# Residual loads with VectorE adds in place of accumulating transfers, and one more seven-product pair, in the down projections of a YOCO trunk

## The chip, the cores and the metric

The kernel runs on one core of a Trainium2 chip. The metric is the device time of one execution in microseconds. Before the change the median of three runs is 2191.21 us (2190.79 to 2191.95). PE is TensorE, DVE is VectorE, ACT is ScalarE, POOL is GpSimd and SP is SyncE, whose queue here carries the weights.

## What is computed

A decoder trunk of two layers in float32 over 256 tokens of width 2048: gated linear attention, a gated feed-forward part with a convolution over tokens, shared keys and values, block-sparse attention, and a second feed-forward part. Each part ends with a projection that is added to the residual stream. These four projections (out of 2048 features twice, out of 5632 features twice) are what the change is about:

```python
h = h + gla_mixer(...)          # ends with  o @ w_out
h = h + conv_ffn(...)           # ends with  (jax.nn.silu(a) * u) @ w_down
h = h + moba_mixer(...)         # ends with  o @ w_out
h = h + conv_ffn(...)
```

## The kernel before

**Weights.** All weights come from DRAM once, in chunks of 1 MB (tile `wraw`, three buffers, requested on SP at L96). A chunk is used in halves of 128x1024. ACT casts each half to its high part `whi` (L140), DVE subtracts to get the low part `wlo` (L141). Each product is then three matmuls: high by high, low activations by high weights, high activations by low weights. `WeightStream.prefetch` keeps the split a few halves ahead of PE; a new chunk is requested when DVE has made the last low part of an older one.

**Down projections.** `down()` is called four times: `go` (the mixer's output), `dn0`, `mo` and `dn1`. Each call makes two column blocks of 1024 (b = 0, 1), and each block walks pairs of 128-row slices of the activations in the order that `ORDERS` gives. A plain pair takes eight 128x512 products, which are 24 matmuls. A pair marked with `+` takes seven products (21 matmuls) of combined operands, as in Strassen's scheme, into seven partial sums p1 to p8 (p[1], p[5], p[6], p[7] serve all four quarters of the result). For it, DVE makes the sums `t13` and `t24` of a chunk's quarters (`_sums`, L106 to L108), four halves (one of them 512 wide) are split in place of two, and the activations need a combination `comb`: a sum of the pair's rows (L613), four steps of 128x128 (L603 to L606), and a split by ACT (L303) and DVE (L304). Combinations are made once for both blocks. For dn0 and dn1 those of pairs 1, 3, 5, 7 are made while the pairs themselves are; the others are made in the first block that needs them, queued two pairs ahead.

**End of a block.** The pairs behind the `|` are plain and come last, first for the left 512 columns, then for the right ones (f = 0, 1). When the last seven-product pair is done, ACT copies p[1] and DVE makes the four sums that all quarters share (`r[0]` to `r[3]`, named c0 to c3, L756 to L760). Then four transfers on POOL's queue add the residual from DRAM to c0 to c3 in place (L762, `accum_op`, 256 KB each; from `x_tok` for go, from `rows1` to `rows3` for the others). During the tail, as each f is finished, DVE adds the last partial sums (L771) and `done` stores the rows (L784, on POOL; for dn1 the output, L834 on SP and ACT).

**What sets the order.** The program is laid out by a scheduler that models time; `with ws.behind()` places what is issued inside it behind the latest split. Buffers of kind `slot` come from one pool of 35 (a place of 4 KB per partition).

Of the kernel before, what the change touches and what calls it, by code (L numbers as in the profile page):

```python
# [8 lines left out]
F32 = mybir.dt.float32  # L9
# [3 lines left out]
OP = mybir.AluOpType  # L13
# [24 lines left out]
def _order(text):  # L38

    words = text.replace("|", " ").split()  # L40
    return [(int(k.rstrip("+")), k.endswith("+")) for k in words], len(text.split("|")[1].split())
# [2 lines left out]
EARLY = (1, 3, 5, 7)  # L44
ORDERS = {
    "go": [_order("0 1+ 2 3+ 4 | 5 6 7"), _order("0 2 1+ 3+ 4 | 5 6 7")],
    "dn0": [_order("0 2 4 6 8 1+ 10 3+ 12 5+ 14 7+ 16 9+ 17 11+ 18 13+ 15 | 19 20 21"),
            _order("0 2 4 6 1+ 8 3+ 10 5+ 12 7+ 14 9+ 16 11+ 13+ 18 15+ 17+ 19 | 20 21")],
    "mo": [_order("0 2 1+ 3+ 4 | 5 6 7"), _order("0 2 1+ 3+ 4 | 5 6 7")],
    "dn1": [_order("0 2 4 6 8 1+ 10 3+ 12 5+ 14 7+ 16 9+ 17 11+ 18 13+ 15 | 19 20 21"),  # L50
            _order("0 1+ 2 3+ 4 5+ 6 7+ 8 9+ 10 11+ 12 13+ 14 15+ 16 17+ 18+ | 19 20 21")],
}

# [104 lines left out]
def trunk(ctx: ExitStack, tc: tile.TileContext, xT, x_tok, cst, msk, w1p, w2a, w_k, w_qa, w_v2, w_v, w_g, w_go,  # L158
          w_up0, w_dn0, w_kk, w_kv, w_mq, w_mo, w_up1, w_dn1, rel, onehot, out):
    nc = tc.nc  # L160
    V, A, T = nc.vector, nc.scalar, nc.tensor
# [11 lines left out]
    def slot(shape, dt, name):  # L173
        return big.tile(shape, dt, name=name, tag="slot")

    def temp(name, shape=(128, 2, S), dt=F32):
        return tmp.tile(list(shape), dt, name=name, tag="temp")

    def bank(name, shape):
        return mis_ps.tile(list(shape), F32, name=name, tag="bank")  # L180
# [5 lines left out]
    ws = WeightStream(tc, raw, parts)  # L186
# [85 lines left out]
    def step():  # L272
        due = [job for at, job in later if at <= cur[0]]
        later[:] = [(at, job) for at, job in later if at > cur[0]]
        for job in due:
            job()
        halves_ = ws.get(cur[0])
        cur[0] += 1
        return halves_
# [331 lines left out]
    def combine_parts(k, xs, into):  # L611
        t = temp("whole")
        V.tensor_add(t, xs[k][:, :, :S], xs[k][:, :, S:])  # L613
        combine(k, [(t[:, i, :128], t[:, i, 128:]) for i in range(2)], into)
# [87 lines left out]
    def down(name, xs, combos, res, done, jobs):  # L702

        for b, (order, n_tail) in enumerate(ORDERS[name]):
            new = [k for k, seven in order if seven and k not in combos]
            todo = {i: list(js) for i, js in jobs.get(b, {}).items()}
            for k in new:
                at = next(i for i, (k_, _) in enumerate(order) if k_ == k)
                todo.setdefault(max(at - 2, 0), []).append(lambda k=k: combine_parts(k, xs, combos))
            low = acc_ps.tile([128, 2, 512], F32, name="acc")  # L710
            pair, single = ((3, 8), (2, 4)) if name.startswith("dn") else ((2, 3), (4, 8))
            p = {n: low[:, i] for i, n in enumerate(pair)}
            p.update({n: bank(f"p{n}", (128, 512)) for n in single})
            left = dict.fromkeys(range(1, 9), 0)
            for k, seven in order:
                for n in ((1, 5, 7, 6, 4, 3, 2) if seven else (2, 3, 4, 8, 2, 3, 4, 8)):
                    left[n] += 3
            begun = set()

            def prods(*todo):  # L720

                w = step()
                for n, _, _ in todo:
                    if n not in p:
                        two = acc_ps.tile([128, 2, 512], F32, name="acc")
                        p.update({n: two[:, 0], {1: 6, 5: 7}[n]: two[:, 1]})
                for xi, wi in ((0, 0), (1, 0), (0, 1)):
                    for n, x, f in todo:
                        left[n] -= 1
                        T.matmul(p[n], x[xi], w[wi][:, 512 * f:512 * f + 512], start=n not in begun, stop=left[n] == 0)  # L730
                        begun.add(n)

            def part(k, i, t):
                x = xs[k][:, i, 128 * t:]
                return x[:, :128], x[:, S:S + 128]

            def comb(k, f):
                return combos[k][:, f, 0], combos[k][:, f, 1]

            last = max(i for i, (k, seven) in enumerate(order) if seven)  # L740
            for i, (k, seven) in enumerate(order[:-n_tail]):
                for job in todo.get(i, ()):
                    job()
                if seven:
                    prods((1, part(k, 0, 0), 0))
                    prods((3, comb(k, 3), 0), (2, part(k, 1, 0), 1))
                    prods((5, comb(k, 0), 0), (7, comb(k, 2), 1))
                    prods((6, comb(k, 1), 0), (4, part(k, 1, 1), 1))
                else:
                    for a in range(2):  # L750
                        prods(*((n, part(k, a, t), f)
                                for n, t, f in ((2, 0, a), (3, 0, 1 - a), (4, 1, a), (8, 1, 1 - a))))
                if i == last:

                    r = [temp(f"c{n}", (128, 512)) for n in range(4)]
                    A.copy(r[0], p[1])  # L756
                    V.tensor_add(r[1], r[0], p[6])  # L757
                    V.tensor_add(r[2], r[1], p[7])
                    V.tensor_add(r[1], r[1], p[5])
                    V.tensor_add(r[3], r[2], p[5])  # L760
                    for n in (0, 2, 1, 3):
                        nc.gpsimd.dma_start(r[n], res(n // 2, 2 * b + n % 2), accum_op=OP.add)  # L762
            for f, ns in enumerate(((2, 4), (3, 8))):
                for i, (k, _) in enumerate(order[-n_tail:]):
                    for job in todo.get((f, i), ()):
                        job()
                    prods(*((n, part(k, a, t), a) for a in range(2) for t, n in enumerate(ns)))
                if f:
                    ws.prefetch(cur[0])
                for t, n in enumerate(ns):  # L770
                    V.tensor_add(r[2 * t + f], r[2 * t + f], p[n])  # L771
                    done(t, 2 * b + f, r[2 * t + f])
# [41 lines left out]
    def middle(name, xs, combos, res, nrm, keep_row, at, feature_major, parked=None):  # L814
        done, back, in_acc, in_bank = onward(nrm, keep_row, parked)
        jobs = {}
        for q, (b, i) in enumerate(at):
            jobs.setdefault(b, {}).setdefault(i, []).append(lambda q=q: back(q, in_acc))
        down(name, xs, combos, res, done, jobs)
        for q in range(len(at), NP):  # L820
            after(1 if feature_major else q - 3, lambda q=q: back(q, in_bank))
        after(2 if feature_major else 3, nrm.close)
        if feature_major:
            after(3, nrm.weave)
# [7 lines left out]
    def last_down(hid, sums):  # L832
        def done(t, c, x):
            (A if t and c % 2 else nc.sync).dma_start(out[t, :, 512 * c:512 * c + 512], x)  # L834

        down("dn1", hid, sums, rows3, done, {})
# [149 lines left out]
    for g in range(4):  # L986
# [4 lines left out]
        f = (q8[:, g % 2 * 4:g % 2 * 4 + 4], (q1[:, 0:2], q1[:, 2:4]))  # L991
# [3 lines left out]
    for g in range(4):  # L995
# [3 lines left out]
        f = (k8[:, g % 2 * 4:g % 2 * 4 + 4], [slot([128, 2, 2, S], F32R, f"k1{c}") for c in range(2)])  # L999
# [120 lines left out]
```

## Time and profile before

| what | before |
|---|---|
| median of three runs | 2191.21 us |
| profiled execution | 2188.61 us |
| its span | 2186.7 us |
| PE busy | 2170.4 us, 99% |
| DVE busy | 1597.0 us, 73% |
| ACT busy | 1284.1 us, 59% |
| POOL busy | 300.9 us, 14% |
| granted TensorE clock, mean | 0.999 |

The profiled execution takes about 2 us beyond its span and is 2.6 us shorter than the median. A matmul's row reads 0.39 us, but matmuls overlap, so the distance of their starts is what one costs. A busy share is a mean over stages: what stands still, and when, is read from the waits and the timeline. Lines are those of the kernel before.

### The profile page before, as it was taken

To read this page: it belongs to the slowest core of one execution; us is meant where nothing else is said; L and a number is where in the kernel's file an instruction comes from. 1 tells how busy PE (TensorE), PEld (TensorE's weight loads), DVE (VectorE), ACT (ScalarE), POOL (GpSimd) and SP (SyncE) were. 2 spreads that over 40 slices of the span, in tenths; PEclk is the share of its full clock that TensorE was granted. 3 is DMA by queue.
4 is the path that set the end of the run, shared out by engine and by line. 5 is a ranking of instruction groups with operands and counts; after the bars stand their busy time and mean duration, and the time that the engine had idled before them with its cause. 6 is when DMAs were issued, how large, how long until landed. Compare 5 with 4: busy or idle time off the path is not lost.

```text
span 2186.7 us, 26956 instructions
## 1 busy us (share of the span) xinstructions
PE 2170.4 (99%) x9693; PEld 1793.1 (82%) x9693; DVE 1597.0 (73%) x2202; ACT 1284.1 (59%) x1858; POOL 300.9 (14%) x448
## 2 busy tenths in 40 slices
PE   9999999999999999999999999999999999999999
PEld 7888887888888888788888888888888888887887
DVE  6655586667776777878967787776777676769887
ACT  6555765556565656555556676555656565655454
POOL 1011111111111111000023241011111111110000
PEclk9999999999999999999999999999999999999999
DMA  8466577577777787675678887676687777775655
GB/s 317 178 231 210 185 245 256 201 241 232 240 240 242 242 256 234 198 251 202 223 252 269 275 277 229 205 235 230 232 249 236 247 237 246 237 243 206 222 205 173
DMA packets 92248, 510.11 MB, mean 233 GB/s; under 512 B 13729, under 2 KB 14769, under 8 KB 42194
## 3 DMA queue, kind: packets, MB, share of 16 engines
q1 hardware_dynamic: 60722, 417.53, 54.4%
q0 software_dynamic: 30816, 90.28, 15.3%
q8 instruction: 76, 1.25, 0.2%
q10 hardware_dynamic: 576, 0.58, 0.1%
q14 instruction: 58, 0.48, 0.1%
HBM read 463.22 MB, written 45.11 MB: 232 GB/s over the span
## 4 chain that ended last, share of the span: by engine, by line
PE 85%; DMA 5%; DVE 4%; issue 4%; ACT 1%; POOL 1%; DVEq 0%; SPq 0%; ACTq 0%; POOLq 0%
PE acc L290 41%; PE acc L293 20%; PE acc L730 13%; PE p L730 9%; DVE wlo L141 2%; DMA wraw<-w_dn 1%; DMA upT<-turned 1%; DMA wraw<-w_go 1%; ACT whi L140 1%; POOL upT L667 1%; DMA turned<-z 0%; PE sT L561 0%; DMA h<-xT 0%; PE o L578 0%; DVE au L680 0%
## 5 line engine op out<-in xcount | busy, mean ns | idle before, releaser
L141 DVE TENSOR_TENSOR wlo<-wraw,whi 128x1024 fp32r<-128x1024 f32 (+1 forms) x786 | 929.7, 1190 | 398.5 <-ACT whi L140 376.7
L140 ACT CAST whi<-wraw 128x1024 fp32r<-128x1024 f32 (+1 forms) x786 | 797.2, 1026 | 604.9 <-PE acc L290 391.0
L290 PE MATMUL acc<-whi,xw 128*128 128x512 f32 x3840 | 952.9, 390 | 2.6 <-ACT whi L140 1.9
L290 PEld LDWEIGHTS acc<-whi,xw 128*128 128x128 f32 x3840 | 719.5, 188 | 154.8 <-ACT whi L140 3.8
L293 PE MATMUL acc<-wlo,xw 128*128 128x512 f32 x1920 | 514.2, 389 | 0.0
L293 PEld LDWEIGHTS acc<-wlo,xw 128*128 128x128 f32 x1920 | 360.3, 188 | 74.8
L730 PE MATMUL p<-whi,hid 128*128 128x512 f32 x572 | 204.0, 390 | 0.0
L730 PE MATMUL acc<-whi,hid 128*128 128x512 f32 x506 | 168.8, 389 | 0.0
L676 ACT ACTIVATE au<-upT,cs 128x256 f32<-128x256 f32 x176 | 96.0, 595 | 70.1 <-DMA upT<-turned 70.1
L140 ACT CAST whi<-t 128x1024 fp32r<-128x1024 f32 x82 | 85.5, 1052 | 87.5 <-PE p L730 26.8
L667 POOL DMA_DIRECT2D upT<-turned x176 | 114.3, 656 | 148.7 <-DMA turned<-z 59.5
L290 PE MATMUL acc<-whi,xkv 128*128 128x512 f32 x512 | 128.8, 391 | 0.0
L661 POOL DMA_DIRECT2D turned<-z x44 | 34.1, 776 | 676.7 <-DVE z L657 615.0
L730 PEld LDWEIGHTS p<-whi,hid 128*128 128x128 f32 x572 | 107.4, 188 | 22.7 <-ACT whi L140 0.4
L680 DVE SCALAR_TENSOR_TENSOR au<-upT,cs,au 128x255 f32<-128x255 f32 x176 | 77.4, 471 | 55.8 <-ACT au L676 55.6
L730 PEld LDWEIGHTS acc<-whi,hid 128*128 128x128 f32 x506 | 95.0, 188 | 19.6
L730 PE MATMUL acc<-whi,comb 128*128 128x512 f32 x328 | 107.6, 393 | 3.4 <-ACT whi L140 3.1
L290 PEld LDWEIGHTS acc<-whi,xkv 128*128 128x128 f32 x512 | 94.6, 188 | 18.7
L730 PE MATMUL p<-wlo,hid 128*128 128x512 f32 x286 | 106.4, 391 | 2.6 <-DVE wlo L141 2.6
L141 DVE TENSOR_TENSOR wlo<-t,whi 128x1024 fp32r<-128x1024 f32 x82 | 98.6, 1217 | 9.8 <-ACT whi L140 5.4
L730 PE MATMUL acc<-wlo,hid 128*128 128x512 f32 x253 | 92.2, 389 | 0.0
L762 POOL DMA_DIRECT2D c<-rows x24 | 21.3, 1074 | 463.4 <-DVE c L757 451.2
(251 smaller groups left out, 1956.3 us busy)
## 6 DMA issues: line engine op xcount, KB each, us to landing
wraw<-w_up SPq DMA_DIRECT2D x176, 1024.0 KB, 5.3
wraw<-w_dn SPq DMA_DIRECT2D x88, 1024.0 KB, 4.9
turned<-z POOLq DMA_DIRECT2D x44, 512.0 KB, 3.5
upT<-turned POOLq DMA_DIRECT2D x176, 128.0 KB, 5.0
wraw<-w_g SPq DMA_DIRECT2D x16, 1024.0 KB, 5.0
wraw<-w_go SPq DMA_DIRECT2D x16, 1024.0 KB, 5.4
wraw<-w_mq SPq DMA_DIRECT2D x16, 1024.0 KB, 6.6
wraw<-w_kk SPq DMA_DIRECT2D x16, 1024.0 KB, 6.0
```

What stands on the lines that cost most here:

```text
L140: one = nc.scalar.copy(hi[:, a:b], src[:, a:b])
L141: two = nc.vector.tensor_sub(lo[:, a:b], src[:, a:b], hi[:, a:b].bitcast(F32))
L290: T.matmul(ps[:, t, :], xs(kt)[:, x0 + 128 * t:x0 + 128 * t + 128], hi[:, c:c + 512], start=kt == 0 and x0 == 0, stop=False)
L293: T.matmul(ps[:, t, :], xs(kt)[:, 128 * t:128 * t + 128], lo[:, c:c + 512], start=False, stop=kt == KT - 1)
L661: nc.gpsimd.dma_start(turned[J].rearrange("(a i) r q c -> (i r) a (q c)", a=4), z.rearrange("p (a q) t c -> p a (q t c)", a=4))
L667: nc.gpsimd.dma_start(f[32 * q:32 * q + 32].rearrange("p a (i c) -> p (a i) c", i=4), turned[J][:, :, q, :].rearrange("a r c -> r a c"))
L676: A.activation(au[:, i, :], t[:, i, :], AF.Identity, bias=col(cb + n), scale=col(cw + 2 * 2 * FT + n))
L680: V.scalar_tensor_tensor(au[:, i, 1:], t[:, i, :S - 1], col(cw + 2 * FT + n), au[:, i, 1:], op0=OP.mult, op1=OP.add)
L730: T.matmul(p[n], x[xi], w[wi][:, 512 * f:512 * f + 512], start=n not in begun, stop=left[n] == 0)
L762: nc.gpsimd.dma_start(r[n], res(n // 2, 2 * b + n % 2), accum_op=OP.add)
```

## The change

It does two things. In the first blocks of dn0 and dn1 the orders end with `13+ 19 15+ | 20 21` in place of `13+ 15 | 19 20 21`: pair 15 takes seven products in the first block too, and pair 19 moves from the tail to the middle. In all eight blocks the four accumulating transfers go; two buffers `kept` receive the residual by four plain loads on POOL's queue, and DVE adds them to c0 to c3, two adds at each f, placed behind the latest split during the first tail pair.

```diff
--- before.py
+++ after.py
@@ -44,10 +44,10 @@
 EARLY = (1, 3, 5, 7)
 ORDERS = {
     "go": [_order("0 1+ 2 3+ 4 | 5 6 7"), _order("0 2 1+ 3+ 4 | 5 6 7")],
-    "dn0": [_order("0 2 4 6 8 1+ 10 3+ 12 5+ 14 7+ 16 9+ 17 11+ 18 13+ 15 | 19 20 21"),
+    "dn0": [_order("0 2 4 6 8 1+ 10 3+ 12 5+ 14 7+ 16 9+ 17 11+ 18 13+ 19 15+ | 20 21"),
             _order("0 2 4 6 1+ 8 3+ 10 5+ 12 7+ 14 9+ 16 11+ 13+ 18 15+ 17+ 19 | 20 21")],
     "mo": [_order("0 2 1+ 3+ 4 | 5 6 7"), _order("0 2 1+ 3+ 4 | 5 6 7")],
-    "dn1": [_order("0 2 4 6 8 1+ 10 3+ 12 5+ 14 7+ 16 9+ 17 11+ 18 13+ 15 | 19 20 21"),
+    "dn1": [_order("0 2 4 6 8 1+ 10 3+ 12 5+ 14 7+ 16 9+ 17 11+ 18 13+ 19 15+ | 20 21"),
             _order("0 1+ 2 3+ 4 5+ 6 7+ 8 9+ 10 11+ 12 13+ 14 15+ 16 17+ 18+ | 19 20 21")],
 }
 
@@ -752,19 +752,25 @@
                                 for n, t, f in ((2, 0, a), (3, 0, 1 - a), (4, 1, a), (8, 1, 1 - a))))
                 if i == last:
 
+                    kept = [slot([128, 2, 512], F32, "kept") for _ in range(2)]
+                    for f in range(2):
+                        for t in range(2):
+                            nc.gpsimd.dma_start(kept[f][:, t], res(t, 2 * b + f))
                     r = [temp(f"c{n}", (128, 512)) for n in range(4)]
                     A.copy(r[0], p[1])
                     V.tensor_add(r[1], r[0], p[6])
                     V.tensor_add(r[2], r[1], p[7])
                     V.tensor_add(r[1], r[1], p[5])
                     V.tensor_add(r[3], r[2], p[5])
-                    for n in (0, 2, 1, 3):
-                        nc.gpsimd.dma_start(r[n], res(n // 2, 2 * b + n % 2), accum_op=OP.add)
             for f, ns in enumerate(((2, 4), (3, 8))):
                 for i, (k, _) in enumerate(order[-n_tail:]):
                     for job in todo.get((f, i), ()):
                         job()
                     prods(*((n, part(k, a, t), a) for a in range(2) for t, n in enumerate(ns)))
+                    if i == 0:
+                        with ws.behind():
+                            for t in range(2):
+                                V.tensor_add(r[2 * t + f], r[2 * t + f], kept[f][:, t])
                 if f:
                     ws.prefetch(cur[0])
                 for t, n in enumerate(ns):
```

The scheduler moves instructions with it. On POOL, at the end of go's first block (`turned<-gates` is the last load before it, `rows_2415` the store of the block's result; c_2585 to c_2588 are c0 to c3), before:

```order
L393 DMA turned<-gates 32x4x256 x4
L762 DMA c_2585<-x_tok 128x512
L762 DMA c_2586<-x_tok 128x512
L762 DMA c_2587<-x_tok 128x512
L762 DMA c_2588<-x_tok 128x512
L784 DMA rows_2415<-c_2585 128x512
L784 DMA rows_2415<-c_2587 128x512
L784 DMA rows_2415<-c_2588 128x512
L784 DMA rows_2415<-c_2586 128x512
L762 DMA c_2942<-x_tok 128x512
```

and now (c_2591 to c_2594 are c0 to c3):

```order
L393 DMA turned<-gates 32x4x256 x4
L758 DMA kept<-x_tok 128x512 x4
L790 DMA rows_2415<-c_2591 128x512
L790 DMA rows_2415<-c_2593 128x512
L790 DMA rows_2415<-c_2594 128x512
L790 DMA rows_2415<-c_2592 128x512
L758 DMA kept<-x_tok 128x512 x4
```

The loads don't wait for DVE's sums any more and stand right behind `turned<-gates`; those of the second block stand right behind the stores of the first, with nothing of DVE's second block ahead of them.

On DVE, in the tail of go's first block (t_2662 and t_2663 are t13 and t24 of the second block's first seven-product pair), before:

```order
L141 TENSOR_TENSOR wlo<-wraw,whi 128x1024
L771 TENSOR_TENSOR c_2585<-c_2585,acc 128x512
L771 TENSOR_TENSOR c_2587<-c_2587,p_2421 128x512
L141 TENSOR_TENSOR wlo<-wraw,whi 128x1024
L771 TENSOR_TENSOR c_2588<-c_2588,p_2422 128x512
L106 TENSOR_TENSOR t_2662<-wraw 128x1024
L141 TENSOR_TENSOR wlo<-wraw,whi 128x512
L107 TENSOR_TENSOR t_2663<-t_2662,wraw 128x512
L771 TENSOR_TENSOR c_2586<-c_2586,acc 128x512
L141 TENSOR_TENSOR wlo<-wraw,whi 128x1024
```

and now (t_2666 and t_2667):

```order
L141 TENSOR_TENSOR wlo<-wraw,whi 128x1024
L773 TENSOR_TENSOR c_2591<-c_2591,kept 128x512
L773 TENSOR_TENSOR c_2593<-c_2593,kept 128x512
L141 TENSOR_TENSOR wlo<-wraw,whi 128x1024
L777 TENSOR_TENSOR c_2591<-c_2591,acc 128x512
L777 TENSOR_TENSOR c_2593<-c_2593,p_2421 128x512
L141 TENSOR_TENSOR wlo<-wraw,whi 128x1024
L773 TENSOR_TENSOR c_2592<-c_2592,kept 128x512
L773 TENSOR_TENSOR c_2594<-c_2594,kept 128x512
L106 TENSOR_TENSOR t_2666<-wraw 128x1024
L777 TENSOR_TENSOR c_2594<-c_2594,p_2422 128x512
L141 TENSOR_TENSOR wlo<-wraw,whi 128x512
```

The four adds of `kept` have come in (L773), two ahead of the first final adds (L777, before L771) and two behind the low part that follows them.

On DVE, in the first block of dn0, where combinations are made beside the splits (t_7195 and t_7196 are t13 and t24 of one chunk, t_7274 and t_7275 of the next), before:

```order
L141 TENSOR_TENSOR wlo<-t_7195,whi 128x1024
L685 TENSOR_TENSOR au<-au 128x256
L604 TENSOR_TENSOR comb<-comb,whole 128x128
L141 TENSOR_TENSOR wlo<-t_7196,whi 128x1024
L106 TENSOR_TENSOR t_7274<-wraw 128x1024
L141 TENSOR_TENSOR wlo<-wraw,whi 128x1024
L606 TENSOR_TENSOR comb<-whole,comb 128x128
L141 TENSOR_TENSOR wlo<-wraw,whi 128x1024
```

and now (t_7207 and t_7208, then t_7286):

```order
L141 TENSOR_TENSOR wlo<-t_7207,whi 128x1024
L685 TENSOR_TENSOR au<-au 128x256
L604 TENSOR_TENSOR comb<-comb,whole 128x128
L141 TENSOR_TENSOR wlo<-t_7208,whi 128x1024
L613 TENSOR_TENSOR whole<-hid 128x512
L106 TENSOR_TENSOR t_7286<-wraw 128x1024
L141 TENSOR_TENSOR wlo<-wraw,whi 128x1024
L606 TENSOR_TENSOR comb<-whole,comb 128x128
L141 TENSOR_TENSOR wlo<-wraw,whi 128x1024
```

A further sum of a pair's rows (L613, pair 15) stands between the low part of `t_7208` and the sum for the next chunk; its four small steps follow among the next splits.

## Rows read from the trace of the kernel before

**Rows 1.** Busy time, share of the span and instructions of each engine.

```profile
PE 2170.4 (99%) x9693; PEld 1793.1 (82%) x9693; DVE 1597.0 (73%) x2202; ACT 1284.1 (59%) x1858; POOL 300.9 (14%) x448
```

**Rows 2.** TensorE's waits: engine, line, waited for; us in total, times, longest us.

```profile
PE acc L730 <- ACT whi L140: 3.1, 1, 3.1
PE p L730 <- DVE wlo L141: 3.1, 4, 0.9
```

**Rows 3.** Timeline (start us, us, engine, line, operation; idle before), TensorE, tail of dn0's first block.

```profile
966.33 1.98 PE L730 MATMUL p<-whi,hid 128*128 128x512 f32 x8
...
969.05 1.98 PE L730 MATMUL p<-whi,hid 128*128 128x512 f32 x8
```

**Rows 4.** Groups by form: busy us, mean ns of one; idle before; VectorE.

```profile
L106 DVE TENSOR_TENSOR t<-wraw 128x1024 f32<-128x1024 f32 x41 | 50.0, 1220 | 27.5 <-DMA wraw<-w_dn 22.9 <-DMA wraw<-w_mo 3.1 <-DMA wraw<-w_go 1.3
...
L613 DVE TENSOR_TENSOR whole<-hid 128x512 f32<-128x512 f32 x11 | 7.5, 684 | 0.0
...
L603 DVE TENSOR_TENSOR comb<-whole 128x128 f32<-128x128 f32 x11 | 3.1, 284 | 1.9 <-DMA out_dram<-c 1.9
```

**Rows 5.** Timeline, VectorE, ScalarE and TensorE, first block of dn0, around 918 us.

```profile
917.37 1.23 DVE L106 TENSOR_TENSOR t<-wraw 128x1024 f32<-128x1024 f32 x1 [0.29 <-DMA wraw<-w_dn]
918.51 1.22 DVE L141 TENSOR_TENSOR wlo<-t,whi 128x1024 fp32r<-128x1024 f32 x1
...
917.19 1.05 ACT L140 CAST whi<-t 128x1024 fp32r<-128x1024 f32 x1 [4.19 <-DVE t L108]
...
918.73 0.39 PE L730 MATMUL acc<-whi,comb 128*128 128x512 f32 x1
```

**Rows 6.** Windows, first block of dn0: stretch, its length, VectorE busy (instructions), clock, DMA.

```profile
895.00:955.00 60.00, 58.98 (x75) 1.00 0.57 210
955.00:970.00 15.00, 10.82 (x12) 1.00 0.68 235
```

**Rows 7.** DMA queues, 318 to 330 us, then 330 to 340: packets, MB, share.

```profile
q0 software_dynamic: 576, 1.05, 55.2%
q1 hardware_dynamic: 217, 1.57, 31.3%
...
q0 software_dynamic: 320, 1.05, 27.0%
```

**Rows 8.** DMA queues 323 to 326 us; timelines of SyncE and ScalarE, first chunk.

```profile
q0 software_dynamic: 221, 0.40, 86.2%
...
322.59 0.33 SPq L96 DMA_DIRECT2D wraw<-w_go  x1
...
331.04 1.05 ACT L140 CAST whi<-wraw 128x1024 fp32r<-128x1024 f32 x1 [7.12 <-DMA wraw<-w_go]
```

**Rows 9.** Timelines of VectorE, SyncE, ScalarE, TensorE, between go's blocks.

```profile
329.06 0.69 DVE L771 TENSOR_TENSOR c<-c,acc 128x512 f32<-128x512 f32 x1 [3.61 <-PE acc L730]
...
332.12 1.23 DVE L141 TENSOR_TENSOR wlo<-wraw,whi 128x1024 fp32r<-128x1024 f32 x1 [1.78 <-ACT whi L140]
...
338.04 0.33 SPq L96 DMA_DIRECT2D wraw<-w_go  x1
...
345.36 0.62 ACT L140 CAST whi<-wraw 128x512 fp32r<-128x512 f32 x1 [4.70 <-DMA wraw<-w_go]
...
349.91 0.50 PE L730 MATMUL acc<-whi,comb 128*128 128x512 f32 x1 [3.12 <-ACT whi L140]
```

**Rows 10.** Windows, TensorE's granted clock (PEclk) behind the wait in go.

```profile
350.00:355.00 5.00, 4.88 (x14) 0.66 0.42 144
```

**Rows 11.** Timelines of SyncE, VectorE and TensorE, dn1, first to second block.

```profile
2050.76 0.33 SPq L96 DMA_DIRECT2D wraw<-w_dn  x1
...
2059.92 1.23 DVE L106 TENSOR_TENSOR t<-wraw 128x1024 f32<-128x1024 f32 x1 [3.64 <-DMA wraw<-w_dn]
...
2081.14 0.50 PE L730 MATMUL p<-wlo,hid 128*128 128x512 f32 x1 [0.81 <-DVE wlo L141]
```

**Rows 12.** DMA issues: KB each, median us to landing, chunks of the down weights.

```profile
wraw<-w_dn SPq DMA_DIRECT2D x88, 1024.0 KB, 4.9
```

## The prediction

> **What bounds the kernel now.** I read the busy shares first, then TensorE's waits, then the stretches around them. TensorE (PE) is busy 2170.4 of 2186.7 us, VectorE (DVE) 73% of the span [rows 1]. So a matmul taken out is worth its slot, and anything else pays only where PE stands still. PE's waits are few: 3.1 us once for a cast on ScalarE (ACT) and 3.1 us in four waits for a low part that DVE makes [rows 2], all of them in the down blocks, which are what is edited. Durations are those of the profiled execution (2188.61 us, of which 2186.7 are the span). The median of the runs is 2191.21, so I work out a difference and set it on the median.
>
> **1. Two plain pairs become seven-product pairs.** Each saves 24 - 21 = 3 matmuls, and the pair is walked once in dn0 and once in dn1: six matmuls. A row of a matmul reads 0.39 us, but rows overlap. In the tail of dn0's first block half a pair has 8 matmuls on high weights, the first at 966.33, then 4 on low ones, and the next half begins at 969.05 [rows 3]: 12 in 2.72 us, 0.227 us each. Six are **-1.36 us**, certain as long as PE is fed.
>
> What feeds them is dearer. By form DVE takes 0.68 us for a pass over 128x512 (the sum of a pair's rows, say), 0.28 for each of the four small steps of a combination and 1.22 for a pass over 128x1024 [rows 4]; in a row each starts some 0.08 us before the one ahead has ended (917.37 and 918.51 [rows 5]), so they count as 0.60, 0.20 and 1.14. The combination of pair 15, with its low part of 512, is 0.60 + 4 x 0.20 + 0.60 = 2.0 us. It leaves the second block and comes into the first. The seven-product form adds the sums t13 and t24 (1.14 + 2 x 0.60 = 2.3 us) and two more low parts, one of them short (1.14 + 0.60 = 1.7). How close PE is there: the high part that began at 917.19 on ACT, right after DVE had made its source, was ready at 918.24, and PE read it at 918.73, 0.49 us later [rows 5]. Of the combination, 0.60 + 3 x 0.20 = 1.2 us stand on DVE ahead of the halves that PE takes at 918 to 920. DVE has 0.29 us of idle just before, at 917.37, and in all 1.02 us in the 60 from 895 to 955, then 4.18 in 15 [rows 6], so I expect 0.9 us of lateness against 0.49 of cushion: +0.4 to +0.5 us, with 0 (the scheduler's order hides it) and +1.4 (all of it, and a little more) as bounds. Twice: **+1.0 us** (0 to +2.8). For the rest of this extra work I count nothing: the plain tail pairs need only two low parts in 5.4 us of PE, and the 4.2 idle us of 955 to 970 are their cover. If that cover isn't enough, rival B follows.
>
> **2. Accumulating transfers become plain loads and DVE adds.** Eight blocks exchange four transfers for four. The price per MB on the rings: from 318 to 330 us the four accumulates of go's first block are the 1.05 MB of the software queue, 55.2% of 12 us, 6.6 us on every ring; from 330 to 340 plain transfers of the same 1.05 MB cost 27.0% of 10 us, 2.7 us [rows 7]. So 8 MB cost some 31 us less ring time. Almost none of that is on the path: none of PE's waits names such a transfer. The 32 new adds are 0.60 us each, 2.4 us a block. Where they count:
>
> **go, first to second block.** The chain is: the chunk asked for at 322.59 moved nothing while the accumulates ran (from 323 to 326 the only packets are the 221 of the software queue), and its cast began at 331.04, 8.4 us later [rows 8]. DVE then worked without a gap from 332.12 until it freed a buffer; the next chunk was asked for at 338.04, and its cast began at 345.36, after ACT had waited 4.70 us for it; PE stood still for 3.12 us until 349.91 [rows 9]. In the next 5 us PE had a granted clock of 0.66 [rows 10], between its two levels of 1.2 and 2.4 GHz, which costs 5 x 0.34 = 1.7 us. Afterwards:
> - The first chunk lands 2 to 3 us sooner. DVE can use 1.8: in the new order the two final adds, which wait for PE until 329.06 [rows 9], stand ahead of the low part, so that it starts at 329.06 + 2 x 0.60 = 330.3 in place of 332.12. -1.8.
> - Of the four residual adds two fall into the idle 3.61 us before 329.06, two into the full stretch: +1.2. The next request comes at about 337.4.
> - The residual loads of the second block stand on GpSimd's queue right behind the last store, so they are issued at about 337 to 339 and fill the rings beside the critical chunk: 0 if they come after it, 2.7 us if all come first. I take the middle, +1.4: the rows that bound it don't say who goes first.
>
> Sum -1.8 + 1.2 + 1.4 = **+0.8 us** (-0.6 to +2.1; I stretch it to +3, since the first block's loads now fall into 306 to 318, where the rings already carry weights). The slow clock stays.
>
> The rows thus show a chunk that got no turn for three microseconds while accumulates were queued [rows 8]. The Trainium skill (DMA: Bandwidth & Descriptors, Queues, rings and completion order) says otherwise: an engine takes turns, one packet each, between the queues that have work. By that rule a chunk (217 packets for 1.57 MB, so 9 per ring and MB) would wait behind 9 plain packets of 0.135 us (27.0% of 160 us over 320), an estimate of 1.2 us, and this term would be +0.6 and not +0.8; the same rule would have let the chunk of 322.59 through, which the trace contradicts, so I keep the middle of the bounds.
>
> **mo, first block.** The same edit; its boundary has one of the four short waits, none of which is longer than 0.9 us [rows 2]. **+0.2 us**, bounds -1.3 (the wait and the steps around it go) and +1.5 (as in go, without its gain).
>
> **dn1, second block.** The accumulates of the first block hold the chunk asked for at 2050.76: DVE stands idle for it 3.64 us, until 2059.92, and is still late at 2081.14, where PE stops 0.81 us [rows 11]. With plain loads the chunk should land in about 5 us, the median of these chunks [rows 12]: **-0.8 us** (bounds -1.0 and 0; other work of DVE may keep it late).
>
> **No cost:** GpSimd's shorter issues (14% busy); the last adds of dn1, which still wait for PE's last product. If the loads came too late there, DVE's last add would show it.
>
> Sum: -1.36 + 1.0 + 0.8 + 0.2 - 0.8 = **-0.2 us**, 2188.4 for the profiled execution and **2191.0** beside the median.
>
> **Rivals.**
> A, the stall in go goes away. If the chunk asked for at 337.4 lands in 4.9 us, as chunks of the down weights do in the median [rows 12], it is there at 342.3; 4.6 us later (345.3 to 349.9) PE gets it, at 346.9, and its old block ended at 349.91 - 3.12 = 346.8 [rows 9]. Then 3.12 + 1.7 = 4.8 us go in place of +0.8: -0.2 - 5.6 = -5.8, **2185.4**. For it: the rings are nearly idle just before. Against it: 1 MB of loads is put in the same three microseconds.
>
> B, DVE becomes the bound of the first down blocks (slower). Combination 2.0, sums 2.3, low parts 1.7, adds 2.4: 8.4 us of new work against 1.02 + 4.18 = 5.2 us of idle from 895 to 970 [rows 6]. If PE's cushions there are used up, DVE ends 3.2 us late, and PE with it: 2 x (3.2 - 0.5) = +5.4 us more, +5.2 in all, **2196.4**. It decides once the lateness passes the cushion of the halves after 930. Against it: a good part of the work comes after 955, where plain pairs ask little of DVE.
>
> C, the loads of the second blocks all go before the critical chunks, in go (+2.1) and mo (+1.5): +1.3 + 1.3 more, +2.4 in all, **2193.6**: no visible change.
>
> D, the edit does nothing that shows, since PE is never short of work: -1.36 alone, 2189.9. It can't be told from the forecast.
>
> **The numbers.** A measurement of this kernel can tell 0.2%, 4.4 us: below 2186.8 is faster, above 2195.6 slower. Forecast with C and D: 0.72, spread by the bounds over 2187 to 2195.5, a little of it beyond. A: 0.15. B: 0.13. Faster 0.18, same 0.67, slower 0.15. The range goes from 2186.0 (into A) to 2195.5.
>
> **What would show it.** In the profile after: 9687 matmuls on PE in place of 9693; plain packets where the accumulates were and no weight chunk above 8 us beside them; PE's wait for ACT in go between 2.5 and 5 us, with the slow clock behind it; a wait of about half a microsecond for ACT or DVE near 919 and near 2004; no wait at 2081. Wrong would be: the gap in go gone (A), several waits for DVE between 930 and 980 (B), or a slow clock in a stretch that had none.

## The result and the profile after

The changed kernel takes 2207.64 us in the median of nine runs (2195.45 to 2215.67), the kernel before 2191.21. The ratio is 1.0071, 95% interval 1.0053 to 1.0088: slower by 0.7%. Forecast were 2191.0 us, no visible change. The profiled execution takes 2204.61 us, its span is 2202.8. The page of the changed kernel has against [rows 1]:

```profile
PE 2177.1 (99%) x9687; PEld 1794.0 (81%) x9687; DVE 1624.4 (74%) x2244; ACT 1288.9 (59%) x1862; POOL 291.4 (13%) x448
```

Six matmuls are gone, as forecast, and yet PE is busy 6.7 us longer, in part because a matmul at the slow clock is a longer row (0.79 us at 324.50 below, where the row at 320.47 before reads 0.39). TensorE's waits in the changed kernel, to be read beside [rows 2] (us in total, times, longest):

```profile
PE acc L730 <- ACT whi L140: 5.5, 5, 3.3
PE p L730 <- DVE wlo L141: 4.6, 4, 3.0
PE acc L730 <- ACT go L303: 4.1, 1, 4.1
PE acc L290 <- ACT whi L140: 3.7, 7, 0.9
```

The third didn't exist before, the second has a single wait of 3.0 where the longest was 0.9. Where the time went shows best when the same instruction is looked up in both timelines of TensorE. Before (the last row of [rows 9], at 349.91, is the first product of pair 1+ in go's second block, which has walked pairs 0 and 2 by then; then the first products of the first up projection and of dn0, one early in dn0's first block and one early in mo):

```profile
384.12 2.00 PE L290 MATMUL acc<-whi,xw 128*128 128x512 f32 x8
...
865.08 0.39 PE L730 MATMUL p<-whi,hid 128*128 128x512 f32 x1
...
901.83 0.50 PE L730 MATMUL p<-wlo,hid 128*128 128x512 f32 x1 [0.87 <-DVE wlo L141]
...
1398.49 0.50 PE L730 MATMUL p<-wlo,ox 128*128 128x512 f32 x1 [0.53 <-DVE wlo L141]
```

After, the same five:

```profile
357.08 0.50 PE L730 MATMUL acc<-whi,comb 128*128 128x512 f32 x1 [3.28 <-ACT whi L140]
...
391.06 2.00 PE L290 MATMUL acc<-whi,xw 128*128 128x512 f32 x8
...
875.58 0.39 PE L730 MATMUL p<-whi,hid 128*128 128x512 f32 x1
...
912.00 0.50 PE L730 MATMUL p<-wlo,hid 128*128 128x512 f32 x1 [0.88 <-DVE wlo L141]
...
1414.63 0.49 PE L730 MATMUL p<-wlo,ox 128*128 128x512 f32 x1 [0.53 <-DVE wlo L141]
```

They are late by 7.2, 6.9, 10.5, 10.2 and 16.1 us, and the span is 16.1 us longer. So go loses 7.2 us up to pair 1+ of its second block and wins back 0.2, the first up projection loses 3.6, dn0 and what follows it up to mo 5.6, and from mo's first block to the end nothing is lost or won.

**go.** The timelines of GpSimd, SyncE, ScalarE and TensorE in the changed kernel, and below them the clock behind the wait (stretch, length, TensorE busy, clock, DMA share, GB/s):

```profile
307.66 2.18 POOL L758 DMA_DIRECT2D kept<-x_tok  x4
...
312.61 0.33 SPq L96 DMA_DIRECT2D wraw<-w_go  x1
...
313.32 2.00 ACT L140 CAST whi<-wraw 128x1024 fp32r<-128x1024 f32 x2 [2.18 <-DMA wraw<-w_go]
318.94 1.05 ACT L140 CAST whi<-wraw 128x1024 fp32r<-128x1024 f32 x1 [3.62 <-DMA wraw<-w_go]
...
321.94 1.05 ACT L140 CAST whi<-wraw 128x1024 fp32r<-128x1024 f32 x1 [1.47 <-DVE c L761]
322.89 0.90 ACT L493 ACTIVATE g<-turned,cs 128x256 f32<-128x256 f32 x2
323.82 0.62 ACT L303 CAST go<-g 128x512 fp32r<-128x512 f32 x1
...
324.50 0.79 PE L730 MATMUL acc<-whi,go 128*128 128x512 f32 x1 [4.12 <-ACT go L303]
```

ScalarE and TensorE at the same place before:

```profile
317.24 1.06 ACT L140 CAST whi<-wraw 128x1024 fp32r<-128x1024 f32 x1 [0.96 <-DMA wraw<-w_go]
...
319.13 0.62 ACT L303 CAST go<-g 128x512 fp32r<-128x512 f32 x1
...
320.47 0.39 PE L730 MATMUL acc<-whi,go 128*128 128x512 f32 x1
```

The clock after:

```profile
324.00:331.00 7.00, 6.50 (x16) 0.53 0.45 158
```

The loads are issued at 307.66, where the chunks for the next pairs are on their way. From 312 to 315 us the weight queue alone filled the rings before; after, it shares them with the loads (packets, MB, share of 16 engines). Before, then after:

```profile
q1 hardware_dynamic: 167, 1.24, 101.5%
```

```profile
q0 software_dynamic: 178, 0.57, 71.5%
q1 hardware_dynamic: 48, 0.38, 31.4%
```

Less than a third of the weights came through. The chunk asked for at 312.61 took 9.2 us to land; before, one asked for at 312.17 took 5.0. After, then before:

```profile
wraw<-w_go SPq DMA_DIRECT2D x1, 1024.0 KB, 9.2
```

```profile
wraw<-w_go SPq DMA_DIRECT2D x1, 1024.0 KB, 5.0
```

It landed at 321.8, and the cast of it stands at 321.94 (its row names L761 of VectorE, which ended just then too). What PE needs next, the cast of an activation (`go`, 323.82), is queued behind that cast and begins without idle time as soon as ScalarE gets to it. Before, the same cast began at 319.13 and was done at 319.75, 0.7 us before PE used it at 320.47; after, PE starts within 0.1 us of its end. PE stands still for 4.12 us, then runs 7 us at 0.53 of its clock, almost all of it at the lower of the two levels: 7 x 0.47 = 3.3 us, together 7.4.

**dn0, second block.** Here the loads are issued when their buffers come free, at 1069.89. Timelines of GpSimd, SyncE, VectorE and TensorE, then the clock:

```profile
1069.89 2.14 POOL L758 DMA_DIRECT2D kept<-rows  x4 [43.84 <-PE acc L730]
...
1072.23 0.33 SPq L96 DMA_DIRECT2D wraw<-w_dn  x1
...
1080.88 1.23 DVE L106 TENSOR_TENSOR t<-wraw 128x1024 f32<-128x1024 f32 x1 [1.87 <-DMA wraw<-w_dn]
1082.03 0.68 DVE L108 TENSOR_TENSOR t<-wraw,t 128x512 f32<-128x512 f32 x1
1082.63 1.22 DVE L141 TENSOR_TENSOR wlo<-wraw,whi 128x1024 fp32r<-128x1024 f32 x1
...
1083.90 0.50 PE L730 MATMUL p<-wlo,hid 128*128 128x512 f32 x1 [2.97 <-DVE wlo L141]
```

```profile
1083.00:1089.00 6.00, 5.10 (x15) 0.72 0.67 247
```

The same pattern with VectorE: the chunk asked for at 1072.23 is late (its sum begins 8.7 us behind the request), that sum (L106) stands at the head of VectorE's queue, and the low part that PE waits for, 1082.63, comes behind it.

### The profile page after: what moved, and what is told of

The parts are those of the page before. It is cut to its first block, busy times and chain, and to the rows that moved or that the text cites. A ratio compares the mean times of both kernels' runs of the same rounds, so it can differ in the third digit from the quotient of the medians.

```text
span 2202.8 us, 27013 instructions
## 1 busy us (share of the span) xinstructions
PE 2177.1 (99%) x9687; PEld 1794.0 (81%) x9687; DVE 1624.4 (74%) x2244; ACT 1288.9 (59%) x1862; POOL 291.4 (13%) x448
## 4 chain that ended last, share of the span: by engine, by line
PE 80%; DMA 6%; DVE 6%; issue 5%; ACT 2%; POOL 1%; SPq 0%; DVEq 0%; ACTq 0%; POOLq 0%
PE acc L290 37%; PE acc L293 19%; PE acc L730 13%; PE p L730 9%; DMA upT<-turned 3%; DVE wlo L141 3%; ACT whi L140 1%; DMA wraw<-w_dn 1%; POOL upT L667 1%; DMA wraw<-w_go 1%; DMA turned<-z 1%; DMA w2s<-w2a 0%; DVE t L106 0%; PE sT L561 0%; PE o L578 0%
## 5 line engine op out<-in xcount | busy, mean ns | idle before, releaser
L730 PE MATMUL acc<-whi,comb 128*128 128x512 f32 x344 | 112.8, 394 | 5.7 <-ACT whi L140 5.5
L141 DVE TENSOR_TENSOR wlo<-t,whi 128x1024 fp32r<-128x1024 f32 x86 | 103.7, 1218 | 6.2 <-ACT whi L140 3.3
L730 PEld LDWEIGHTS acc<-whi,comb 128*128 128x128 f32 x344 | 64.9, 189 | 22.6 <-ACT whi L140 8.8
```

The costliest lines, as they stand in the source:

```text
L141: two = nc.vector.tensor_sub(lo[:, a:b], src[:, a:b], hi[:, a:b].bitcast(F32))
```

## The experiments

Theory L: the plain loads, issued early, take ring time from weight chunks at places where ScalarE's or VectorE's queue is headed by work on such a chunk. Rivals: D, VectorE has too much to do in the first down blocks; S, the two buffers or the adds cost; and that ring time costs anywhere.

Each letter is one comparison, with its own runs of the kernel before; times are compared within a letter.

| run | median us (before beside it) | ratio, 95% interval |
|---|---|---|
| e1, orders alone | 2195.39 (2192.08) | 1.0013, 1.0002 to 1.0024 |
| e2, residual alone | 2197.65 (2192.08) | 1.0032, 1.0017 to 1.0047 |
| e3, no loads | 2189.33 (2192.08) | 0.9993, 0.9980 to 1.0005 |
| e4, loads after the sums | 2199.05 (2192.08) | 1.0027, 1.0012 to 1.0041 |
| f1, the change again | 2206.45 (2191.70) | 1.0055, 1.0037 to 1.0074 |
| f2, loads in go and mo | 2198.43 (2191.70) | 1.0024, 1.0007 to 1.0041 |
| f3, loads in dn0 and dn1 | 2191.10 (2191.70) | 0.9988, 0.9971 to 1.0005 |
| f5, loads without adds | 2209.02 (2191.70) | 1.0064, 1.0039 to 1.0089 |
| g1, orders, loads in dn0 and dn1 | 2198.63 (2189.52) | 1.0037, 1.0023 to 1.0051 |
| g2, orders, loads in dn's first blocks | 2191.68 (2189.52) | 1.0012, 1.0004 to 1.0020 |
| g3, loads in all but go | 2188.60 (2189.52) | 0.9997, 0.9987 to 1.0007 |
| g4, go and mo, loads after the sums | 2193.01 (2189.52) | 1.0013, 1.0003 to 1.0022 |

**e1, the orders alone.** The second hunk of the change is left out.

> Only the two orders of the change; the residual stays with the four accumulating transfers. Theory L (the plain loads, issued early, take the rings from the weight chunks that ScalarE and VectorE wait for in order): the orders are innocent, 2189 to 2193 us, and go shows its old wait of 3 us near 350 and no wait near 320. Theory D (VectorE has too much to do with the extra seven-product pair): most of the loss is here, 2198 us or more, with waits of TensorE for VectorE between 900 and 980.

Measured 2195.39, between the two. go is as L says: no wait near 320. Theory D's waits between 900 and 980 aren't there: the 0.88 us at 904.24 is as before. Where the orders do lose time is something that neither theory named. Timelines of VectorE and TensorE in this run:

```profile
985.38 0.69 DVE L771 TENSOR_TENSOR c<-c,p 128x512 f32<-128x512 f32 x1 [3.07 <-DMA c<-rows]
...
991.21 0.73 PE L730 MATMUL p<-whi,hid 128*128 128x512 f32 x2 [1.83 <-DVE c L771]
...
1077.66 0.50 PE L730 MATMUL p<-wlo,hid 128*128 128x512 f32 x1 [2.06 <-DVE wlo L141]
```

With two tail pairs in place of three the accumulating transfers land too late; the final adds wait for them, and PE waits for the partial sums they hold. And near 1078, in the second block, a low part is late: 2.06 us, with the clock at 1.00 behind it (1077 to 1083).

**e2, the residual alone.** The first hunk is left out.

> The loads and adds of the change with the old orders. Theory L: nearly the whole loss, 2200 to 2210 us, with the wait of 4 us for ScalarE's cast of go near 320. Theory D: less than half of it, 2192 to 2197 us.

Measured 2197.65, 5.6 us over before, with a wait of 3.5 us for the cast of go near 324, and no wait at all between 1000 and 1100, although the loads are issued at 1067.63. That is below the range of L and just above that of D. The two parts of the change cost more together (16.4 us) than one by one (3.3 and 5.6).

**e3, no loads.** The loads are left out, and the buffers are filled with zeros instead, so that the adds stay:

```diff
-                        for t in range(2):
-                            nc.gpsimd.dma_start(kept[f][:, t], res(t, 2 * b + f))
+                        nc.gpsimd.memset(kept[f], 0.0)
```

> The changed kernel, but the two buffers are filled with zeros by GpSimd at the place of the loads, so that the residual of the four projections is left out and 8 MB of loads with it; the buffers, adds and orders stay. Theory L: the loss goes, 2186 to 2192 us, no wait near 320 and none near 1084. Theory S (the two buffers per block, taken early out of the pool of 35, or the adds on VectorE, are what costs): it stays, 2200 us or more.

Measured 2189.33: S and D fall. Everything else of the change (orders, buffers, adds) costs nothing that can be measured once the loads are out. L's sign is only nearly met: waits of 1.4 us for the cast of go near 322 and of 1.0 near 1071 are left.

**e4, loads after the sums.** The loads of the change are taken out where they stood and put here:

```diff
                     V.tensor_add(r[3], r[2], p[5])
+                    for f in range(2):
+                        V.tensor_copy(kept[f][:, :, :1], r[3][:, :2].rearrange("p (t c) -> p t c", c=1))
+                        for t in range(2):
+                            nc.gpsimd.dma_start(kept[f][:, t], res(t, 2 * b + f))
```

> The changed kernel, but each buffer first gets two columns of the last shared sum, so that its loads are issued when that sum is done, where the accumulating transfers were issued before. Theory L, in the form that the place of the loads decides: go's wait near 320 is gone and the time is 2187 to 2196 us. If the loads cost wherever they stand (ring time alone), it stays at 2200 us or more.

Measured 2199.05: neither. The wait of go near 324 falls to 1.34 us, as L says, but in dn0's first block VectorE now waits for the loads in the short tail, 2.93 us at 993.26. PE has no wait there, so this doesn't say what e4 loses. PE waits 1.94 us at 902.92 and 1.86 at 1016.38, each with a slow clock behind it (0.66 from 905 to 910, 0.60 from 1018 to 1022), and 1.61 at 1086.44. What makes these waits isn't shown.

**f1, the change again.**

> The changed kernel again, beside the following three on one chip: 2200 to 2212 us, with a wait near 320 and one near 1080 that end the same way as in the first profile. If either wait is chance, it is missing here.

Measured 2206.45. Both waits are there, 3.86 us near 324 and 3.3 near 1082.

**f2 and f3, loads by place**, with the old orders; `plain` chooses between the two kinds of transfer:

```diff
+                    plain = name in ("go", "mo")
+                    if plain:
                         kept = [slot([128, 2, 512], F32, "kept") for _ in range(2)]
...
+                    if not plain:
+                        for n in (0, 2, 1, 3):
+                            nc.gpsimd.dma_start(r[n], res(n // 2, 2 * b + n % 2), accum_op=OP.add)
```

> Old orders; plain loads and adds in go and mo alone, accumulating transfers in dn0 and dn1. Theory L puts most of the 6 us of the residual part here, since go's wait near 320 with the slow clock behind it is worth 5 to 7 us: 2195 to 2200 us. If the loads of dn0 and dn1 carry it, 2190 to 2194 us.

> Old orders; plain loads and adds in dn0 and dn1 alone. Theory L: with the old orders nothing near 1080 is late enough for the loads to matter, 2189 to 2193 us, about the kernel before. If the loads cost by themselves wherever they are, 2195 us or more.

Measured 2198.43 and 2191.10. With the old orders the cost comes with the loads of go and mo, and the loads of dn0 and dn1 are free (g3 below takes mo out too). In f2 PE waits in go as after the change, and by the end of go it is late by 4.2 us; about as much again, 3.9, is lost in the up projection behind it. TensorE in f2:

```profile
322.99 0.50 PE L730 MATMUL acc<-whi,go 128*128 128x512 f32 x1 [2.69 <-ACT go L303]
```

**f5, loads without adds.** The four lines of the adds (L770 to L773 of the change) are left out.

> The changed kernel without the 32 adds of the loaded rows, so the residual is left out; the loads stay. Theory L: the loads alone carry the loss, 2200 us or more. If the adds are what makes the loads bite (VectorE has to wait for them), 2187 to 2195 us.

Measured 2209.02, as much as the whole change: the loads carry it.

**g1 and g2, the orders with loads in dn alone.** `plain = name in ("dn0", "dn1")`, in g2 with `and b == 0`.

> Both orders and the plain loads and adds in dn0 and dn1; go and mo keep the accumulating transfers. Theory L: go has no wait for its own cast near 320 beyond 2 us, the wait near 1080 stays at 3 us or more with the slow clock behind it: 2194 to 2199 us, 8 to 12 less than the whole change. If go isn't the main place, 2201 us or more.

> Both orders; plain loads and adds only in the first blocks of dn0 and dn1, whose tail the orders make short; accumulating transfers elsewhere. Theory L, with its second part (a short tail doesn't cover accumulating transfers, a busy second block doesn't cover loads): no wait for them near 990 and 2082, about 1 to 2 us near 1075: 2189 to 2193 us. If the orders cost by VectorE's work, 2195 us as with the orders alone.

Measured 2198.63 and 2191.68. VectorE, then TensorE, in g1, whose loads were issued at 1060.19:

```profile
1073.52 1.23 DVE L106 TENSOR_TENSOR t<-wraw 128x1024 f32<-128x1024 f32 x1 [4.21 <-DMA wraw<-w_dn]
...
1076.54 0.80 PE L730 MATMUL p<-wlo,hid 128*128 128x512 f32 x1 [5.31 <-DVE wlo L141]
```

and TensorE in g2, which has no loads there:

```profile
1073.65 0.50 PE L730 MATMUL p<-wlo,hid 128*128 128x512 f32 x1 [1.01 <-DVE wlo L141]
```

So with the new orders PE waits 1 to 2 us in the second block of dn0, and with loads in it 3 to 5 us, with a slow clock behind them in the change. With plain loads in the first blocks, behind the shorter tail, e1's wait near 991 is gone; but g2 is still 2.2 us above before, so a gain from them isn't shown.

**g3, loads in all but go.** `plain = name != "go"`, old orders.

> Old orders; plain loads and adds in dn0, mo and dn1, accumulating transfers in go. Theory L: 2188 to 2192 us, at or a little below the kernel before; mo has shown no difference between the two kinds of transfer. If mo's loads cost, 2194 us or more.

Measured 2188.60, ratio 0.9997: not to be told from the kernel before. So the loads of mo, dn0 and dn1 are free with the old orders.

**g4, go and mo, loads after the sums.** As f2, with the loads where e4 has them.

> Old orders; as in f2, plain loads in go and mo, but issued when the last shared sum is done. Theory L: the wait near 320 falls to 0 to 2 us and the time to 2190 to 2194 us, against 2198 with the loads at their early place. If the loads' place is not what costs, it stays at 2197 us or more.

Measured 2193.01: 3.5 us above the kernel before, where f2 is 6.7 above, with 0.87 us of waiting near 322 where f2 has 2.69. The intervals of the two ratios overlap, so the times alone don't settle it; the traces do in part. From go's first product to the first one of pair 1+ in the second block PE takes 63.0 to 65.4 us in the five profiles with early loads in go (the change, f1, e2, f2, f5), 59.5 and 61.2 with late ones (g4, e4), and 58.0 to 62.2 in the seven with accumulating transfers or none. The place of go's loads shows, but by a small margin: the profile before is one of the shortest (58.0), and e3, f3, g1 and g3, without plain loads in go, also wait 1.0 to 1.6 us for the cast of go near 322. So a part of the change's wait there need not be the loads'. Of g4's 3.5 us another part is a wait of 2.31 us in the up projection, at 501.86, with a clock of 0.66 from 502 to 507.

```profile
322.75 0.50 PE L730 MATMUL acc<-whi,go 128*128 128x512 f32 x1 [0.87 <-ACT go L303]
```

## Why the prediction was wrong

By its own steps:

- **Six matmuls, -1.36 us.** The count is right: 9687 on the page. The gain can't be seen behind the losses.
- **VectorE in the first down blocks, +1.0.** Right in kind in dn0: PE waits 0.40 us for ScalarE at 929.48, which is 919.3 by the clock of before ("near 919"). In dn1 it isn't shown: the wait of 0.61 at 2008.15 is at 1992 by that clock, not "near 2004". Rival B didn't come; e3 has all of VectorE's new work and takes 2189.33.
- **go, +0.8 (up to +3).** This step failed: it measured +7.2 in the profiled execution. The part that was worked out, the second wait, came nearly as forecast: the next chunk is asked for 1.1 us earlier by PE's clock (forecast 0.6), its cast begins 8.6 us later in place of 7.3, PE waits 3.28 us in place of 3.12, and the slow clock stays. (In rival A, "its old block ended" at 346.8 is the end of pairs 0 and 2 of the second block; the sum there is the same.) After, SyncE and ScalarE:

```profile
343.94 0.33 SPq L96 DMA_DIRECT2D wraw<-w_go  x1
...
352.52 0.62 ACT L140 CAST whi<-wraw 128x512 fp32r<-128x512 f32 x1 [5.97 <-DMA wraw<-w_go]
```

  But the loads of the first block, which "now fall into 306 to 318, where the rings already carry weights", were given a stretch of a bound and no term of their own. With them came the wait of 4.12 us and the 3.3 us of slow clock. I had asked how far PE was ahead of the halves of weights, and not what else stands in ScalarE's queue behind a cast that waits for a chunk. The cushion that counted, 0.7 us between the cast of go and its use, stood in no term. The sign "no weight chunk above 8 us beside them" failed with it.
- **dn0's second block: no term at all.** I priced its loads by the total ("8 MB cost some 31 us less ring time. Almost none of that is on the path"), and didn't ask where the new place put them. g1 against f3 shows that it takes both edits: new orders and loads there. PE waits 2.97 us and loses 6 x 0.28 = 1.7 to the clock; the 0.40 at 929.48 and two short waits behind it (0.47 and 0.23) add 1.1, and three matmuls fewer take 0.7 off. That is 5.1 of the 5.6 us up to mo.
- **The total itself** was high, since the plain price was read from stores (`rows<-c`, 330 to 340) and not from loads. Over the whole span the software queue's share, times the span, fell from 335 to 311 us: 24 us less, not 31. Before, then after:

```profile
q0 software_dynamic: 30816, 90.28, 15.3%
```

```profile
q0 software_dynamic: 28768, 90.28, 14.1%
```

- **dn1, -0.8.** Not seen: from mo to the end nothing is won, although three matmuls of the -1.36 lie there. The wait at 2081 is gone, but the chunk didn't land "in about 5 us": beside the plain loads it took 9.2, beside the accumulates 9.1. VectorE still stands idle for it, 2.53 us where it was 3.64, and PE has a wait of 1.02 us for ScalarE at 2103.94. VectorE after:

```profile
2079.47 1.23 DVE L106 TENSOR_TENSOR t<-wraw 128x1024 f32<-128x1024 f32 x1 [2.53 <-DMA wraw<-w_dn]
```

- **mo, +0.2.** Right: from its first product to the next projection PE takes 90.8 us, before 90.9, and g3 shows no cost of its loads.
- **The rule on turns.** With plain loads both queues moved in 312 to 315, so there the trace agrees with the Trainium skill (DMA: Bandwidth & Descriptors, Queues, rings and completion order) in that neither queue is shut out. My own estimate of 1.2 us from it was made for the chunk of the second block, where the cast came 1.3 us later behind its request. In the first block, where I made none, the chunks asked for at 309.32 and 312.61 took 9.5 and 9.2 us, those at 308.99 and 312.17 before 5.7 and 5.0.

Of the 16.1 us, 3.6 lie in the first up projection, whose order of products the change doesn't touch and for which the prediction had no term. In the change itself they are several short waits: 0.29 us near 504, four of 0.33 to 0.69 between 679 and 792. A wait near 504 stands in every run with plain loads of go from DRAM (the change twice, e2, e4, f2, f5, g4; 0.29 to 2.79 us) and in none of the others (before, e1, e3, f3, g1, g2, g3). e4 and g4 have it with late loads, so the early place isn't its cause. In f2, where it is longest, GpSimd, ScalarE and TensorE:

```profile
481.79 0.78 POOL L661 DMA_DIRECT2D turned<-z  x1 [16.78 <-DVE au L682]
490.75 2.59 POOL L667 DMA_DIRECT2D upT<-turned  x4 [8.18 <-PE acc L293]
...
502.06 1.10 ACT L676 ACTIVATE au<-upT,cs 128x256 f32<-128x256 f32 x2 [8.68 <-DMA upT<-turned]
...
504.14 3.48 PE L290 MATMUL acc<-whi,xw 128*128 128x512 f32 x8 [2.79 <-ACT whi L140]
```

The load of the turned rows comes 9.0 us behind their store, where it was 5.0 before, and ScalarE waits 8.68 us for them with a cast of weights (503.06) behind it: the pattern of go again. What sets it off isn't settled. The loads of go may do it through what the scheduler makes of the rest, or through the rings; nothing was tried on it alone.

## What to carry to other kernels

A cheaper transfer need not be cheaper at another place. Ask of a transfer that moves earlier which transfers are then in flight, and which in-order queue has work on them at its head; what PE needs may be something else in that queue. A cushion of the weights says nothing of the activations that are cast behind them. Two edits that share a bound have to be priced together: here the shorter tail made the accumulates late, and early loads cost where the next stretch had become tight.

## What was not expected of the hardware

- Four accumulating transfers of 1.05 MB took 6.6 us of every ring and plain stores of the same size 2.7 [rows 7]; over the span the change has 24 us less of such time, and still it is slower, by plain loads at a worse place.
- A wait of 4.12 us was followed by 7 us at a granted clock of 0.53 and cost almost as much again; one of 2.06 us in e1 by none, although two shorter ones in e4 (1.94 and 1.86) were followed by slow stretches. So the length of the wait alone doesn't tell.
- The times of the changed kernel lie between 2195.45 and 2215.67, those of before between 2190.41 and 2196.27 in the same comparison. That small differences in when a chunk lands make this spread is a guess: only the profiled executions have a trace.
